# A new table of ranks for the steps of a one-core GLA and RWKV-7 layer

## The chip, the core and the metric

The kernel runs on one core of one Trainium2 chip. The metric is the device time of one execution in microseconds (us); less is better. The engines are PE (matmuls; PEld is its weight load), DVE (vector), ACT (activations), POOL (GpSimd) and SP, whose queue issues the loads and stores. Each engine works through its own queue in order and waits on semaphores for the others.

## The reference, cut to what matters

One decoder layer on 4096 tokens of width 1024: norm, one projection for two groups of heads, a GLA group and an RWKV-7 group, their gated outputs through one output projection, residual and a final norm.

```python
h = _rmsnorm(x, norm_w)
u = (h @ w_in).astype(f32)
gla_u, rwkv_u = u[..., :GLA_IN], u[..., GLA_IN:]
...  # GLA: chunks of 64 tokens, state S_t = diag(a_t) S_{t-1} + k_t^T v_t, o_t = q_t S_t
o = _gla_chunked(q, k, v, log_a.reshape(B, T, GLA_HEADS, GLA_DK))
gla_out = o.reshape(B, T, GLA_VW) * jax.nn.silu(gg)
...  # RWKV-7: token shift, decay w, rate a, normalised key kk, then the delta rule
#   sa = S (-kk);  S = S * w + sa (kk * a) + v k;  y = S r
y = _rwkv7_scan(r_h, decay.reshape(hs), k_h, v_h, kk, a.reshape(hs))
rwkv_out = (y + bonus.reshape(B, T, RWKV_W)) * jax.nn.silu(rg)
merged = jnp.concatenate([gla_out, rwkv_out], axis=-1).astype(x.dtype)
return x + merged @ w_out          # then _rmsnorm(x, final_norm_w)
```

## The kernel before, in words

The tokens are worked through in 8 blocks of 512, the layer's width in tiles of 128. Nine streams of work (generators, one for each kind) describe all of it:

- x loads a block of tokens (`xr<-in_xT_dram`), squares and sums it on PE (`bank<-gtwo,...`), spreads the factors (`bank<-ident,nyg`) and normalises it on DVE;
- w and the output's weights are split into f16 parts: the largest entry is found by transposes (`identb,amW`) and DVE, the matrix is scaled (`wr<-x,scl,wr`) and stored to DRAM (`wdr`), from where it is loaded again later as `wr`, `wg`, `wo`;
- a does the RWKV projections (`bank<-x,wr`) of a unit (a block and one of 4 pairs of heads, so 32 units) and its decays, and makes the inverse of a triangular matrix for every chunk of 64 tokens. For that the matrix goes by the small tiles `Nb`, `nd`, `f`, `Tc`, `td` through DRAM: `nd<-Nb` stores it, `f<-nd` loads it in another layout, POOL builds the inverse row by row with 31 products and 31 sums (`tm<-Tc,f` and `Tc<-Tc,tm`), `td<-Tc` stores that and `Nb<-td` loads it back;
- i multiplies the blocks of the inverse on PE (`Nb,Ta`);
- c is the chain of states, 8 steps of one chunk for a unit, each of them through PE (`ch`), ACT (`us`, `uv`) and DVE (`sv`); e is the same for the last unit;
- d normalises the chain's output and joins the gate (rows by `bcdc` and the like through DRAM);
- g does the GLA part for two pairs of heads in a block, with the row factors `bcdh`, `gbc`, `ki`, and p its projections (`bank<-x,wg` and `bank<-wg,x`);
- o does the output projection and the last norm.

The kernel is built in two passes. `build` runs the streams, and every instruction (a pair of matmuls by `duo` is one) becomes a step with the steps that it depends on (its operands, buffers and PSUM banks); there are 23,692. The steps' numbers and buffers come from the tables `COUNTS` and `STARTS`, the same before and after. Then the steps are issued in the order of a second table, `ORDER`: it is text of packed numbers, and `order()` (line 403) unpacks it to one rank for each step, a permutation. The step of lowest rank whose predecessors are all issued is issued next:

```python
rank = order()
left, can = [len(s.on) for s in steps], [(rank[s.n], s.n) for s in steps if not s.on]
heapq.heapify(can)
while can:
    s = steps[heapq.heappop(can)[1]]
    ...
    s.f()
    for m in s.to:
        left[m.n] -= 1
        if not left[m.n]:
            heapq.heappush(can, (rank[m.n], m.n))
```

So the table alone sets the order of each engine's queue and of SP's. No time is in it: an engine waits for its next step until the semaphores of that step's predecessors have come. Steps on PE have a form (how many of the array's rows and columns a tile takes, and whether it is f32); the costs that the planner has for a change of form, for POOL's sums beside DVE and for a load's landing stand in functions (`forward`, `backward`, `cost`) that rank the steps ahead of time and aren't called when the kernel is built.

Instructions other than the paired matmuls carry the line of the helper `call` (L844), pairs that of `duo` (L905), so views of the profile are read by tiles and not by lines.

Of the kernel before, what the change touches and what calls it, by code (L numbers as in the profile page):

```python
# [2132 lines left out]
```

## Time and profile before

| what | value |
|---|---|
| time, median of 3 runs | 2143.72 us (2143.46 to 2144.85) |
| the profiled execution's own time | 2145.66 us |
| its span | 2143.8 us |
| instructions | 69142 |
| granted PE clock, mean | 0.995 |
| bytes | 322.31 MB by DMA, 150 GB/s |

The span is what the trace covers, the own time is the whole execution's. A row of a timeline has a start, a length, the engine, the line, the operation, the output and its inputs, and in brackets how long the engine stood idle just before and what ended that. A length on PE has a matmul's whole latency in it, so neighbouring rows overlap. Rows of SP's queue give issues; a transfer lands later.

### The profile page before, as it was taken

What the parts mean: (1) busy time and instruction counts of PE and PEld (TensorE: products, weight loads), DVE (VectorE), ACT (ScalarE), POOL (GpSimd) and SP (SyncE); (2) the same over time, 40 slices, a digit from 0 to 9 for tenths busy, and PEclk for the clock granted to TensorE, in tenths of its full rate; (3) what the DMA queues carried; (4) which work ended last, traced back from release to release, by engine and by line L of the source; (5) the groups of instructions that cost most, each with busy time, mean ns of one, the idle gap of its engine ahead of it and who ended that gap; (6) DMA issues with size and microseconds to landing.
All of it is one profiled execution on the core that took longest, in us unless ns stands there. A gap on an engine that the chain in (4) does not pass through costs nothing.

```text
span 2143.8 us, 69142 instructions
## 1 busy us (share of the span) xinstructions
PE 2093.1 (98%) x27880; PEld 1355.5 (63%) x27880; DVE 1615.3 (75%) x3528; ACT 1278.2 (60%) x3356; POOL 880.3 (41%) x2267
## 2 busy tenths in 40 slices
PE   7999999999999999999999999999999999999898
PEld 5656575566756667567676667656676565755565
DVE  8889988668776787678776776757978588776776
ACT  7778786465654656455755457555565565554562
POOL 3663344562253542626433254443334535344500
PEclk9999999999999999999999999999999999999999
DMA  5757756465344653455534654346534465344442
GB/s 172 232 163 249 219 175 179 129 194 171 95 130 132 198 149 109 121 165 173 146 98 126 181 167 129 95 137 187 178 107 112 143 187 165 101 124 133 126 131 85
DMA packets 273701, 322.31 MB, mean 150 GB/s; under 512 B 129844, under 2 KB 135140, under 8 KB 273380
## 3 DMA queue, kind: packets, MB, share of 16 engines
q1 hardware_dynamic: 273380, 317.89, 50.1%
q8 instruction: 218, 3.57, 0.7%
q14 instruction: 103, 0.84, 0.1%
HBM read 272.74 MB, written 45.05 MB: 148 GB/s over the span
## 4 chain that ended last, share of the span: by engine, by line
PE 79%; DVE 12%; POOL 3%; DMA 2%; issue 2%; ACT 2%; SPq 0%; DVEq 0%; ACTq 0%; POOLq 0%
PE bank L905 63%; PE bank L844 9%; PE ch L905 4%; DVE DD L844 2%; POOL tm L844 2%; PE y L844 1%; POOL Tc L844 1%; PE y L905 1%; DVE bk L844 1%; DVE nva L844 1%; DVE x L844 1%; DVE xr L844 1%; DVE Nb L844 1%; DVE mgg L844 1%; DVE nta L844 1%
## 5 line engine op out<-in xcount | busy, mean ns | idle before, releaser
L905 PE MATMUL bank<-x,wr 128*64 128x512 f16 (+1 forms) x6732 | 830.5, 379 | 5.8 <-ACT wr L844 1.9
L844 POOL TENSOR_TENSOR tm<-Tc,f 128x60 f32<-128x60 f32 (+24 forms) x961 | 345.0, 359 | 581.7 <-DMA f<-nd 462.3
L905 PEld LDWEIGHTS <-wr 128*64 128x64 f16 x6732 | 366.8, 111 | 261.6 <-issue 19.9
L905 PE MATMUL bank<-x,wg 128*64 128x512 f16 x3180 | 393.3, 380 | 2.7 <-DVE amW L844 1.3
L844 POOL TENSOR_TENSOR Tc<-Tc,tm 128x60 f32<-128x60 f32 (+24 forms) x961 | 349.9, 364 | 73.6
L905 PE MATMUL bank<-x,wo 128*64 128x512 f16 x2760 | 325.3, 380 | 0.4 <-ACT x L844 0.4
L844 DVE SCALAR_TENSOR_TENSOR sv<-ch,PC,psd 64x64 f32<-64x64 f32 x434 | 122.6, 283 | 205.9 <-PE ch L905 179.2
L844 POOL TENSOR_TENSOR xacc<-xacc,xr 128x512 f32<-128x512 f32 x98 | 134.5, 1372 | 334.0 <-ACT xr L844 188.5
L905 PEld LDWEIGHTS <-wg 128*64 128x64 f16 x3180 | 175.1, 110 | 130.3 <-issue 4.4
L905 PEld LDWEIGHTS <-wo 128*64 128x64 f16 x2760 | 151.0, 110 | 117.6 <-issue 1.4
L905 PE MATMUL bank<-wg,x 128*64 128x256 f16 x3072 | 197.5, 274 | 4.1 <-DMA wg<-wdr 3.9
L905 PEld LDWEIGHTS <-x 128*64 128x64 f16 x3216 | 172.9, 111 | 20.7 <-issue 4.8
L844 ACT COPY us<-ch 64x64 f32<-64x64 f32 x496 | 101.9, 205 | 134.4 <-PE ch L905 117.4
L844 ACT COPY uv<-ch 64x64 f32<-64x64 f32 x496 | 102.0, 206 | 88.0 <-PE ch L905 80.5
L844 ACT ACTIVATE psd<-sv,PC 128x128 f32<-128x128 f32 x248 | 98.8, 398 | 84.7 <-DVE sv L844 61.5
L844 ACT ACTIVATE sa<-bank,mu_s 128x512 f32<-128x512 f32 x104 | 71.3, 685 | 53.2 <-PE bank L905 47.4
L844 DVE COPY_PREDICATED Nb<-mc,bank 64x512 f32<-64x512 uint8 x128 | 93.0, 729 | 5.8 <-PE bank L844 3.5
L844 DVE COPY_PREDICATED DD<-mc,bank 64x512 f32<-64x512 uint8 x128 | 93.2, 729 | 2.5
L905 PEld LDWEIGHTS ch<-uv,bk 128*64 128x64 f32 x992 | 67.4, 137 | 39.6 <-ACT uv L844 6.6
L905 PEld LDWEIGHTS ch<-sv,DD 128*64 128x64 f32 x992 | 65.6, 136 | 39.3 <-DVE sv L844 13.8
L905 PEld LDWEIGHTS ch<-us,Nb 128*64 128x64 f32 x992 | 66.7, 137 | 37.2 <-ACT us L844 6.5
L905 PE MATMUL ch<-uv,bk 128*64 128x64 f32 x992 | 71.5, 223 | 3.5 <-ACT uv L844 3.2
(359 smaller groups left out, 3538.4 us busy)
## 6 DMA issues: line engine op xcount, KB each, us to landing
wr<-wdr SPq DMA_DIRECT2D x254, 256.0 KB
wg<-wdr SPq DMA_DIRECT2D x182, 256.0 KB
xr<-in_xT_dram SPq DMA_DIRECT2D x176, 256.0 KB
wo<-wdr SPq DMA_DIRECT2D x116, 256.0 KB
f<-nd SPq DMA_DIRECT2D x128, 128.0 KB
x<-in_wt_dram SPq DMA_DIRECT2D x29, 512.0 KB
wdr<-wo SPq DMA_DIRECT2D x17, 512.0 KB
rn<-bcda SPq DMA_DIRECT2D x64, 128.0 KB
```

Source lines behind the costliest of these rows:

```text
L844: put(t0, self.name, d, lag, cols, tiles, tab, outs, ins, lambda: f(*a, **kw))
L905: nc.tensor.matmul(x, lhsT=l, rhs=y, start=start, stop=stop)
```

## The change

The text of `ORDER` is replaced. `COUNTS`, `STARTS`, all steps, their costs, buffers and code are the same. Unpacked and compared for each queue, with the share of steps whose place in the queue is another:

| queue | steps | moved | mean shift, places | largest shift, places |
|---|---|---|---|---|
| PE | 12,968 | 4198 | 1.27 | 108 ahead, 49 back |
| DVE | 3528 | 1561 | 0.87 | 71 ahead, 12 back |
| ACT | 3206 | 1165 | | |
| POOL | 2261 | 252 | | |
| SP (loads and stores) | 1729 | 890 | 1.05 | 12 either way |

On PE the number of neighbours of different form goes from 590 to 589. Places that the text below speaks of, by their times in the profile before:

- 12.08: the first spread of the norm on PE, 5 places later, behind four pairs of statistics.
- 39.5: the DVE step that makes `glr`, 5 places later.
- 1799 to 1805: on SP's queue the four loads `f<-nd` go ahead of `bcdh<-nyg` (1801.18), `gbc<-bcdh` (1802.85), a `wr` load (1803.28) and `ki<-bcdh` (1803.71); the last `nd<-Nb` one place ahead.
- 1978.64: a chain step on PE, ahead by several matmuls.
- 2007.11 and 2010.99: two `wg` loads, each one place back, behind `td<-Tc` (2022.62), which goes two places ahead.
- 2022 to 2023.7: a few matmuls of `wr` from later on are put ahead of those that use the two `wg` loads.

```diff
@@ -55,168 +55,166 @@
 PUT_OFF = 1.0
 FILL = ()
 ORDER = (
-    "c-qZf2b^40)qiE`_L9x+rWevkAPFgu5FnxVCZIF{L7IRcibxYt1mu(AhYA)zQBV+3L{Moef`Sw&A`qmv0D(X
...
+    "c-qx{2bf(|)%Gd3PA{1xGwD5{q(BOU0HKB^y+{>7K;%OO1w=X`A0P+<f&w<Ah@yxnpdbR$1XOyJ4k5HaN
...
```

More of the change, by code (lines that the diff above doesn't have):

```diff
@@ L217 @@
[L217 to L219 removed]
+    "c-qx{2bf(|)%Gd3PA{1xGwD5{q(BOU0HKB^y+{>7K;%OO1w=X`A0P+<f&w<Ah@yxnpdbR$1XOyJ4k5HaNYBjN`OnIE*K^<5*{9sOGxGg;o|Aj$-gD2{XYaLFeb-u(9LMp3qbK<HLU6dj`)ZH6;AjqxRl)T(30^b7"
@@ new lines @@
+    "F*G=C!1ar`XD&E8gU>d_?@Gb@$Ae>0aC8KJcLlG@f@7=TeHLT<cX0SPUw)gzd%0H;?^g%!3n|9wSw4Fr`0e_^Ypvznd~nFU+k@jj!FitL96A0Fe3!vzbMV<D<D7GY<HF#)(ZTB>xbCIF-;?kxw_>hj94)~yFF5YS"
+    "Gs<VL1@GH}SDCxpg7-4t4Z-no@V+K^-6%M8uCkaDc|R4;DDP(k$653oLn7v=2j}?4cQy1`H$AhgTh@5q;q>0eZ}s~zpovkz@jRYU=;aN(ACCDhVvKKMedQdXmmzrnHlAJ1e<gU|7`zS+j`K0LiNW!5@P0Ure?oAK"
+    "1daN5t;d|ne7+T&zd`W2G3M=sfJo)}zJ)Qj(R0c14P56Utl#H@<DTGsC(-R{nopVAeQDq2g8weF?86-PRHb{dsY3eaBLmutJ7-KV);BP|iCBk><vz98H=c0}6M7HkRQCQ+#&|tkOI~*kjwzV46M~a33tsQT+U0Og"
@@ new lines @@
+    "6TX+f8}VMozf*92TX4Zsf_oet{Qbk=b^qXXT5t%Tc`5jQcQ?G}WUT4Q#u{Y$F!#BL&y@~#1&u8PA8V!kQ49Ji;u(+ZC*B;j{x$SIKLFPko<0Vj%?*x!7`%LAJge-jq1b<$;k!@p>_Q{I!CYmr#wthF!#!Mlw;o={"
+    "2S0k%4bNK<9Cw$(b8<NHSld=w=Mng>#_~+cJ7j&n1A3{$eOW&Iz(PMd)~rF_V~H2c1WjH-veND6eXq2f#l7UdcVON<l3B6`rr_LR_?@ibwZXAR@LfxaakNx8?hk3+WDM5_$BDsbEMJ!4oJk3ER|7hD6*|Q4jBA^}"
+    "Q<{4}I8Wr{N5QMei^-t9`6LVF{8_=E^7!3y$eTyK{@tVIF(u}i|0gA1w;kW=hp}w~edM8FE@VFb7R=8h!K>_(D}vV_2d~ctuO~sKvdop=?=3t%_)hlEeC)MfK}Qmu=+DNUlDS_K!52+krGfUl2VKL1uG#^a{9}Cf"
@@ new lines @@
+    "<>37`c#dm&LV2$|O7#wx<k#=}i8t31pWx?^>mMWZ2KqcP;(qh+Te;5dIA=)2y`uQayTR{fLr-!cBlii8n}WaZ$J#{wK128006gfLgt?JDx@~a$nRIzRHUn>N#q~vxx+*xf1pnuAZ;`PY_uB?K-gvCJ=#KI_$TF_>"
+    "3glWg;haY3Ybwu$f4quk?7;7L#@OWip}~KLKsIfU-yIkn7bMJIK4y&T6D>Up+d^f~EzoD>{a}3eQt<jkoG<cc1m3sNb!OnaF?c>7YcdGDQGT}r?K78T+eM(KkHF78>?wKwd@0>NPP2zx3vDDFOCkSU@bb8Gb?w)y"
+    "LLagn*9G@I9P2OhbzE?4271xo502Qgao61p{OvZJ_dWbZ?4@C_n;z%`56d|NE9-2upwCc4pJj;m$>+1N*B>{Y>Ac|Y(;y2<uu%um{`AR5;X*I7J+GI7F86}Iu{&his)YI77IxxR7)u@bMD7fZGw58|FQ3EpbSzs0"
@@ new lines @@
+    "$C-VYQ<=L3{j@&Q>HQ`N>)0Rnn+9E7d8QA3D*S0_cklVGOQ|QXwCEUa3SC<F_MNaTAH;P|gKV2kw*K}ho-J$eGdV<Wx)6Gi_;>!+6Y8IO{zTA56ZEiuVhqRQ-omGw;gfSMwx35jkw?Ct#SyZZb&Cy2R_JH9CeVBa"
+    "^LrH5(X;42a{oUV*BOt!dARZUQu;d&yV(UVu<1!2=1HDU^oy-hu1(xAs2}Kh23`*?mF;60>oL$b7eK!o<(B6t51p(Be60cR#diKnaNLgh6us#%vZYifR=Y-hHDY7clf986KDj&I-vfV}OTJFq9#`3t18-KnKMxw#"
+    "^X6OjoQHGTFvf+@FVqGXT0N!|(x=**hY;^P5V{KQ(FVMVA7XR(>YAZ%HDM2luJ$I4t;Hh8ry8I6DP(@04$)O_!|#Od?h-zabvQDD_v`{1d$A|{Hy(2;Ja4?kzC8l-<Qp=~HdeXjEaUreG;W#e>w|N4gx^Db&ZD89"
@@ new lines @@
+    "|1dc5)9%m?&cat9zr8Yn57>P56Y0K<*z<pf54f3RY!7spS%?`-120ng-xmDxM$r6x(6oH_3$am+Ig{sF82s@y(H9IEVvbYvCZV;hgCCyW9qq623^|j<-q{6ns`gKobUitqhHq43AL|>otn!Hi$!;v-`9^_9=8Um7"
+    ";n-UIqVl^^S%&x+PY?8!8sfoOiopzpUG*~PMLv57e)v|RJsHFKVhcikh&-yLIT&Zm(Q~vGQxbUOv)Cs*FPj?YTt#}6JjWL;-z!g(Ik_D3w7o&E<{qAqQm?Oxu><ZS`&wTAD*On1T=(Ak7I}Fh=1yZM%Cm>k{f@zB"
+    "e=Wtw!F=$CYhZU=g)#XN=gM4P4SsnX_*D<tjC&D%irm?{)H^05V|v`J+(z203R${KKiVH#S;m*f*Y*K)<4rI(FN1Gi(v>bw8F$Ej-@*9ou`2yhYGaCx(G{%WTsPb!r$Qesf)-a3y)<LZeT&{&7onroMa-YZaD=wT"
@@ new lines @@
+    "LbkDAWxB+ONr!kD@j#E{R1fxk3*=)C&$UGS#=&>vXxzhb{(K|e*+RO}P~z<wiVv4a2lBAKd3@eV&t3x`rur=R4Nlk#=ZvH=?-?9>V~^|J9s=HVE#~17(z$12td}E>UaZ1aA57zwYyOMYS7SHR5PO#KormW<m2A<E"
+    "p*MEovqq9V9`Sx1=b`xgFZiAM=uZ$|I_B0Rdpye5q35(3u@;T{z5+ck1E15S&<8y7=SE#~Yv|qb{@9*)ouC$<t+vRJ4D?OKEy!oz1?|qnT-6)DnS*)IvCbmju6daLsGZ;g*)Mqgb@2KX@e!ot4a&=#i4J8R9)ZlC"
+    "f^`&H*u}W!uVDkLPhaHvD@048>+TU8`v%81Wj_R8{H81Xz8!I$pNk$(zl-xhWg~3oiS+(q_<e_9pPdidmAQW?c(Xa_+g^gtVu-QNMiNidx%vWh&RNhGRtgUQw&nYHrY4KMGo7A6Fb}Gyi48v`f%fBk35^N97!Pv9"
@@ new lines @@
+    "jIj(h?z5eR#|XyZ7U+M9e~|d+_hQzL=d;yVH`CTXlH#ik7X9ip@{>=Gz#}y!%-JXlkCb`81GeEe@R`K1u3OpD^9XDX;a`7|*mFQbE5V~=&&>dzS%i6Mf}C0p?_WcVQTF>g!TY&*wkxvsd1@iMneBA(W&AB*HaF%%"
+    "{Y1V$Ao%<GTsW_C%}s*8PtS$>p&8d%pROZz?mpzpx)SlZG4SW8zNz~98pNqHINmL#*Egc{r-HGzrp;W${nyHDgRVq(-Jk4}29o2ogtzG-Kde6MrO;~z<NGG^eXNavL&nC%U0N}(i=lI{{p6Bg%%@{m!aNl~-|CON"
+    "1J_eO-Yyv519-L^WJ6R;{ZgDi#Tb`9OOE7MwR-Z$@G(xrb>~2rkbi3+%l>H0=}?l{;|+|^7<@0!@f&<L7IwetfLZ7cwHA47`f5ztyElbzJ_jB=j(%5<>+0MMCOxQV_=o2N|2;<gM4m_dXg|htYzRKHUmtwrm0&FV"
@@ new lines @@
+    "l=gKk;rP~o=FD@NjX3KZ@L}PN!uy2|z6{wj3w&5&Ya(}Zqz{zvej9h-Vn-teFfR4Y3eV^DItlv0H!%-tdz{x9zTeOd{cCRk2a%)s^85KYUWHxc!Uysn$f_lX0aSDC2FRHXL(YreV|UR0zO-LX4?f!q_aBbuzKHN$"
+    "eHlX*e04;3PmkycFN5ALfKN38{<=TWrQkoW4o=#tE7YTpb^8|c9iP%Cp>dE)jQP%C9yZ1p<@K@z{c1GDI`gz=8z^RA`|T{~FnO{mHUeJxQ1}-%0mkD31J^3{;myGxo0Q7<um-ZD8)3tVZuLm;<!_<)-#WmtW5x3o"
+    "D!_8;`9AG~8J2x##uv;u)_PcTS&yZqvW(cA&KnegA<_8sBKW>N3-8Whj+cRVd<oB(1(xZs;Pn~U62gOjL4MDIg>GhGZB=i{AQmNSc#cI!$n`;Hc@}-!gAelCaz7lK1oUyeA3mGLG2Sq+_Zh5H4|EIm>3W8rMq^~^"
@@ new lines @@
+    "(;jE6+j@jko*4Y->#$X;#a&J?`~_Ls>tc5uKz=2emv3Wl?~n85;`0%>Rs-$3RoGV?lPwbFe?H<0_28iyngfy1$0PPL8T9rG;wuwre)7a48xbeVgB}a;4P8a!Y9Ku*8!=A>L;tJC`i%vxjt1{}x;v!*m4-Yo#`w2t"
+    "Equ5x2K&k55FdrC{dRa(jWaw5Ix5h7kB5J0FfbTXq2Iq9(9cQ0JI%uU{hH>sjqLJkLDPpv(9gUo`Jb%Y_Q80LD24ZVz>W7G)WpnD95%wEbrBjq0W#vUK49n@V`33a6<(``Z07>#Y~P4yXfW=TF=*{v*m<61u57-j"
+    "Vih><IE)*Q)r<H(ZVg`o%}uwg;Y#q&w}ByO55CwBwzcXGzcciY?*xCJN&Ghl9x)sC-v+?Pcri3ug6+K${5h>XIubmg9k@yleB&kf*motq@oa>@Vx$p&ttB5=mT>WE!;ipR=$?He;<`I0j6F{}y=VB2ZS*-6@_Z(~"
@@ new lines @@
+    "?}BghE&Og1jH@2sZBIP88|OF!U~7%<r|TTrhu_RjdEUYBNqd+Jp~-J_hWOX-x*`4i1hVmJ*yxH=mHluk=2CEoN>g{Iw2k8Qqm3>4V-ED2sbVhmnu7VM4~`?;Q2%}%d2l{t(yt62GCZX(+{}%62RS1@$2@tYLz}<-"
+    "6nsSWwpP+ha)!-d8%r1A(v;r_kGdCnjQAQ}qu9x6@a-&kO<jUa%A~O8GVsmiNv~19@m}!xNO}&R{E|ho8(i4Ng5mraIFi%c-uaTAWlTfqUOOAS;uE^xbA-Q|N&I<B$fa!{N7m+DkPofh;*-ok*Xc0UDnpoB7doxb"
+    "!AGUu{?;RnYfi?!eS<b?@cGeXx5|D!trW_W83sMtu!C`H8-?NU2%oVP*7FGby&AOC0=r=Y(Cl#7w3k2!9D}(YhFoB;0{p&btgqrK@5dU>g-qTT`u5uKLdLEpK0nQv%a<U#UHGZjGv-R|p!<p6%r$I^+vxf`S@?ua"
@@ new lines @@
+    "2bWmaHz>#EEYObXv=3r_@`xb`?L8$i7R>J#h__~qeW1Cz--wytMX-N!z}NT||7DK&RJEA)op7y}kv}os4P!$kvbk@kTmw@l^T@VQACB^j$@u(NF>$~RQs_*BVUx7r)lcAkvtSoX?xpx?&VUbh3h}Zv*!#kh&m>)@"
+    "2YhC`|8lMX`xnj6*017v2UK{z?47Id{$=<%YlBG=-Sjof`J?(F*VZ-aBMd{1@rIzOZwBvW@9k*G<toO+lRpFwHx5%$v|#OPA!F`EEc9K_{|e||&thy3Vq7JICZB-cZ8z|Tt!a#!>pc{5nD1+1Fq**&rxI^dfBeTJ"
+    "FXxa?E*mkws-N7{54nFkM120|K;Z4|g}TN)!F$Q?obIm6H@pgSKHFmAI5z~7f0!G}y)OVa(I3yLwDPA?7;DxV4O<Y7QDoFc#_!I9U6zGEMsNl4dO0xP`&58$N)tCY&-h#Pq5BBG!}k6d@>9$sjO3+|X<5QCzZns;"
@@ new lines @@
+    "@htu+*U<Yq$kx0IcKJ+Pe;2YHFM_UhHTkC$JNYztf!gkjb1RZxZxG#k4Zg1<zk)tvH*$Pk<R0-eJw-mV*@jGcm~{S`5o_=d(p9u}3d^GxDEEAD#QuDbV*aYXEDQ!c-Ye6K;%W9upc&hm6^wJd7#S+qw%x$nr;!bQ"
+    "FXa`xkj2cCmcc)->y$D0m<xMrIIW9bV<=%L-=^yhHuhvI{Z4HZ!Cn2;@bzk*p^m53;wy83YpJ7oxB0`~GW3HHMsDMaw04uCbYrOvM0Hx011Fy(pEH*A%#t4793xNjz&!5*9=bE+s?wy+_Ztbka!8eWW)8elWvj^f"
+    "D<$qjpY@QQZOdQe99gZ+GoO4Z!rQh;c#e7_ANoT>SGV~MCSVN)ffv*hHlrQqbb%IUTl`jU4v?OB&;VR>hUK$8VQY;hdYnX9Ni(Ks;+zyCAiB~~!NN;C?rt|3V^s}SU~+J;m$2TlKZao~P95MpVewH-fDOJ0_^4^a"
@@ new lines @@
+    "|A+F{qHsQLjK9h^a-5zCCU{Rb{7m@Nea1brDfILsFjp$`8<a-@!=X5fM#{CT1vXxI=h4Bs{xK8kJL|0upYNmKZ}Hu=0J|zVldV1B`hOpLZ#`V^733GF-tl>S{wC$hECFwo^=vJb@$-#@(VuR}*9~Lr4xi>^By5ao"
+    "_KvK@|6*<D0i(fwsILcaUhE3(hgIaaFHqiRl8w}E_|(}JYM~k!QNEhn`XSF^ZT?y*#Lyq_mg^6w>=hdKU3-3nNAX`Xo}VWkJ=@5IFJf=$-yMekCW}4yj^Vr77QbzW{wd@CAUH>K`fZSh#(9}C{tu~Uh<T`eR!8{)"
+    "{EVt=tTghEbEG@uQux)b0S>JhdXbM@v@F$oDB`&fMIPC<c#gGtcd2(ghIO*6Q?6r}CtW#5`kJiIEx^vmeSQF*vo*~x>uVznnjK`pNvd9^dY|ms-=(Ov66e>@YdwtXoT&PY<ew;RHkb>+LmW$b@CdS9IInmnY+IeL"
@@ new lines @@
+    "BT;fv{0v`%oYGtm{{Bh$l-BloiQrk>BeAhc8PpWxS2VHfHHh2vkj<xg;rC)s%^_ZJKWc|9>4R-7I_SsU;W|hk=Hmxg77tJG6DltGGRnz1JK?$ZfX<}$!z$4ECYHGt`7|GU|7^jlYkgHGT|LN#3UoYMeqFWoed;UB"
+    "87eyQb)0>~rb@upujQv*p?n+(AIR{8d%Ox?can}`i=FHTTQCcGt@&MCm$loFOBwP*$?L?GA)fi?h4^)lo;+vKHKsz|n)TbF;(Cpg6T$xbMG0}iMKS*Vit_FQAtVnjeu)vlSD#uaV~{?gaiqb^=={!ilIu+W!T4V3"
+    "XM5wk)e*IHpN+vvR%$zGzQTI}!K|Mx_wc$HI&Xs^BZ`EtQ@cm}6#If#e7nNE9EC@`p%m5v8|sEwkp+-@J*Xk}c1nA#L_Uv3+GAQ{PQQE3$a_=%q;&Qn>7pwQT%$SmVgz17k9~qKZq1hQ4`%>dHphwXO~Ey?RrmZ5"
@@ L220 @@
+    "249~afuFdG)*>oDLvm=(Mt!Rtft6URtGm5x3^maDE~Q>(W^Pv2f?+aiYU_MmjreJ2DU|W^VQ1{+rt8^NpWt5>J?EQF*zac}JjZ^)@e!`^r&4eGKWkt)`U6+k5u>wv2G)Re@okK}#Mg~{jQ++w=A6pv*JV=V;Cha|"
+    "53uTcKILu<r8#)Zk{|9y@KQ5Zo@>FGF+c7V%k%dt@$`(5S5TzSHvx_zL(imsz(x36|E`5DmL-`~guYlq*RF-m;(_+Gmdqm3D+l8_7#lap(7$rf4T?^=KU^lk#`KN)FkT9~rq;0KGSJN*!L!c5INR_HgCM&HLtbjl"
+    "nKnA_8l0znChJk#qs1xrL&_rlGLrU84e~S!bY2^HH`~mUoZdb2wC4J&M$OvM7W`q0B_GaB$h9_K^A*}^%@~J=`>!M{Q;}+5X^o6!geR1F`hUnTCt?"
 )
```

276 lines of the change are left out of this document (114 added, 162 removed).

## The prediction

> **What bounds the kernel now.** I read the page's first parts, then a table of stretches, then the waits of the matmul engine, then the timeline at the places where the table of ranks moves something.
>
> ```profile
> span 2143.8 us, 69142 instructions
> PE 2093.1 (98%) x27880; PEld 1355.5 (63%) x27880; DVE 1615.3 (75%) x3528; ACT 1278.2 (60%) x3356; POOL 880.3 (41%) x2267
> PE 79%; DVE 12%; POOL 3%; DMA 2%; issue 2%; ACT 2%; SPq 0%; DVEq 0%; ACTq 0%; POOLq 0%
> 0.00:214.00 214.00, 188.93 (x2366) 124.72 (x2368) 183.89 (x473) 163.17 (x349) 100.89 (x252) 0.98 0.66 204
> 214.00:428.00 214.00, 209.28 (x2804) 134.55 (x2800) 176.54 (x398) 141.08 (x376) 95.17 (x251) 1.00 0.59 176
> 428.00:1929.00 1501.00, 1497.28 (x20008) 967.85 (x20006) 1101.92 (x2273) 871.47 (x2332) 630.45 (x1643) 1.00 0.49 144
> 1929.00:2036.00 107.00, 101.05 (x1298) 63.46 (x1294) 75.06 (x161) 49.97 (x144) 50.99 (x119) 0.98 0.45 131
> 2036.00:2090.00 54.00, 53.44 (x810) 36.13 (x808) 41.13 (x126) 36.45 (x112) 0.00 (x0) 1.00 0.48 130
> 2090.00:2143.80 53.80, 43.15 (x614) 28.82 (x610) 36.81 (x102) 16.07 (x46) 2.82 (x4) 0.93 0.26 85
> ```
>
> The first three lines are the span, the busy times and the chain that ended last; the others are stretches with their length, then busy time and instructions of PE, PE's loads, DVE, ACT and POOL, PE's granted clock, the DMA share and GB/s. PE is the bound: idle 2143.8 − 2093.1 = 50.7 us. The stretches say where: 25.1 before 214, 4.7 up to 428, 3.7 in the 1501 us after that, 6.0 up to 2036, 0.6, and 10.7 in the tail. The same instructions run in the new order, so only these 50.7 us and PE's price of changing form are to be had, while a worse order can add idle time anywhere.
>
> ```profile
> PE bank L905 <- DMA wg<-wdr: 4.1, 2, 3.9
> PE ch L905 <- ACT uv L844: 3.2, 4, 1.0
> 187.58 1.09 PE L844 MATMUL bank<-ident,bk 128*128 128x128 f32 x8
> 188.61 0.62 PE L905 MATMUL bank<-x,wr 128*64 128x512 f16 x4
> ```
>
> Two of the waits (total us, times, longest): most are of this kind, a few times under 1 us, spread over producers. The two timeline rows (start, length) show a change of form: from the first of eight transposes to the f16 matmul behind them go 188.61 − 187.58 = 1.03 us, the visit and its two changes together, so one change costs a part of half that; 0.1 us is my estimate.
>
> **The change, part by part.** It replaces one table, the rank of each of the 23,692 steps. Decoded, 4198 of PE's 12,968 steps change place, mean 1.3 places; 1561 of 3528 on DVE, 1165 of 3206 on ACT, 252 of 2261 on POOL and 890 of 1729 loads and stores on SP's queue. Nothing is added or removed. Changes of form on PE go from 590 to 589: **−0.1 us**.
>
> *Start.* The first spread of the norm (from 12.08 below) moves five PE places back, behind four pairs of statistics; by the first row eight such matmuls take 0.60 us. DVE's normalisation waits for it, and behind that lies the weight split that PE waits for at 20.68:
>
> ```profile
> 8.92 0.60 PE L905 MATMUL bank<-gtwo,uv 128*64 128x1 f32 x8 [0.70 <-ACT uv L844]
> 12.08 1.10 PE L905 MATMUL bank<-ident,nyg 128*64 128x128 f32 x8
> 18.92 1.70 DVE L844 SCALAR_TENSOR_TENSOR wr<-x,scl,wr 128x1024 f16<-128x1024 f32 x1
> 20.68 0.64 PE L905 MATMUL bank<-x,wr 128*64 128x256 f16 x4 [1.79 <-DVE wr L844]
> 13.30:20.60 7.30, 5.18 (x70) 4.07 (x70) 7.30 (x21) 5.49 (x14) 2.59 (x4) 1.00 0.94 309
> ```
>
> The split keeps its place on DVE, so the 1.79 us wait grows by 0 to 0.6. I take **+0.5**, near the upper bound, since DVE was busy for all of the 7.30 us before (last row: length, then PE, PE's loads and DVE) and has no gap that swallows it.
>
> *Waits that go.* For each wait of PE I took how far its producer moves ahead (places times the lengths of the steps passed), less PE's own shift, capped by the wait. 22 places give something, 7.5 us in all: 1.3 before 30 us, 1.1 in the chain steps at 136 to 163, 1.6 at 175 to 226, 0.4 at 312, 0.9 between 1307 and 1799, 1.5 at 2010 to 2015, the rest after 2070. One of each of two groups and the largest:
>
> ```profile
> 162.50 0.34 PE L905 MATMUL ch<-uv,bk 128*64 128x64 f32 x4 [0.71 <-ACT uv L844]
> 2010.41 0.34 PE L905 MATMUL ch<-uv,bk 128*64 128x64 f32 x4 [0.65 <-ACT uv L844]
> 2013.77 0.49 PE L844 MATMUL bank<-DD,bk 64*128 64x128 f32 x2 [1.15 <-DVE bk L844]
> ```
>
> The steps around the large waits at 42, 57.6, 153, 158 and in the tail stand as before. A relieved chain step is followed by the next one of the same chain, whose producer is then late instead; so I count two thirds: **−5.0**, bounds 0 and −7.5.
>
> *Waits that come.* The same reckoning the other way finds 20 places (45 links) where a producer falls behind its use on PE, first at 3.7 us, last at 2013.8, 12.8 us in all. The largest two:
>
> ```profile
> 1978.64 0.28 PE L905 MATMUL ch<-us,Nb 128*64 128x64 f32 x4
> 1977.14 0.73 ACT L844 COPY Nb<-bank 32x256 f32<-32x256 f32 x2
> 39.52 0.62 PE L905 MATMUL bank<-glr,guw 128*64 128x512 f16 x4 [0.73 <-DVE pw L844]
> ```
>
> The chain step at 1978.64 moves 1.9 us ahead on PE while the copies that it reads end at 1977.87: about 1.3 us of new wait. At 39.52 the producer on DVE moves five places back: 1.1. I count these whole (2.4). The other 10.4 assume that a producer starts late by all that was put ahead of it; but in the long middle DVE is idle 1 − 1101.92/1501.00 = 27% of the time and ACT 42%, which takes up most shifts of one place. I count a fifth, 2.1. **+4.5**, bounds +1 and +12.8.
>
> *SP's queue at 1800.* SP issues in order, and an entry that isn't ready holds all behind it:
>
> ```profile
> 1799.42 0.43 SPq L844 DMA_DIRECT2D nd<-Nb  x1
> 1801.18 0.57 SPq L844 DMA_DIRECT2D bcdh<-nyg  x1
> 1802.85 0.34 SPq L844 DMA_DIRECT2D gbc<-bcdh  x1
> 1804.23 0.38 SPq L844 DMA_DIRECT2D f<-nd  x1
> 1805.13 3.33 SPq L844 DMA_DIRECT2D f<-nd  x3
> 1807.85 0.75 DVE L844 SCALAR_TENSOR_TENSOR go<-go,gnh,gbc 128x512 f32<-128x512 f32 x1
> 1811.16 0.75 DVE L844 SCALAR_TENSOR_TENSOR gbc<-gbc,gus,gep 128x512 f32<-128x512 f32 x1 [1.11 <-ACT gep L844]
> ```
>
> The four loads of f are moved ahead of bcdh and gbc. The first f issued 4.8 us after the last nd; the last nd goes out at about 1797.9 now, so the f's run from 1802.7 and gbc follows 3 to 5 us later than before. DVE's use at 1807.85 stood 5.0 us after its load; it slips by up to 3.6, of which the idle 1.11 at 1811.16 takes a part: 0 to 2.5 us for the chain step behind it on DVE, of which PE has other matmuls to fill most: **+0.5**.
>
> *SP's queue at 2007.* Here the largest single wait of the late stretch changes hands:
>
> ```profile
> 2007.11 4.20 SPq L844 DMA_DIRECT2D wg<-wdr  x2
> 2022.62 0.37 SPq L844 DMA_DIRECT2D td<-Tc  x1
> 2025.43 0.89 SPq L844 DMA_DIRECT2D wg<-wdr  x2
> 2023.35 3.99 PE L905 MATMUL bank<-wg,x 128*64 128x256 f16 x70
> 2025.92 5.28 DMA wg<-wdr
> 2031.25 2.96 PE L905 MATMUL bank<-wg,x 128*64 128x256 f16 x26 [3.92 <-DMA wg<-wdr]
> 2027.00:2031.00 4.00, 0.33 (x8) 0.06 (x2) 0.26 (x1) 0.00 (x0) 0.00 (x0) 0.96 0.79 241
> 2031.00:2036.00 5.00, 4.75 (x62) 4.28 (x64) 2.83 (x15) 0.22 (x1) 0.00 (x0) 0.69 0.07 14
> ```
>
> The store td of POOL's last sum, ready only at 2022.6, moves ahead of the first two wg loads (2007.11 and 2010.99). They can then go out at 2023.0 and 2023.4, though PE wants them from 2023.4 on, after the few matmuls put ahead. The second two loads still follow at about 2025.6. Two loads issued together took 5.28 us after the second issue, with nd and f beside them; so the first pair lands between 2026 and 2028.7 and PE waits 2.6 to 5.3 us there, then works some 3.7 to 4 us on it (the row at 2023.35) and finds the second pair landed. The old 3.92 us wait goes. The half clock moves with the wait: 0.69 of full speed over 5.00 us is 1.55 us lost once, before and after. Resumed work on the second pair starts between 2029.7 and 2034, against 2031.25: −1.5 to +2.8, and +5 if PE is slowed on both stretches. I take **+0.3**.
>
> *POOL.* Its sums stay whole, with the same steps. By its row (busy us and mean ns; then the idle time before and what ended it) the engine stood idle 462.3 us for loads of f, so a shift there lies beside PE's work except at the store just told:
>
> ```profile
> L844 POOL TENSOR_TENSOR tm<-Tc,f 128x60 f32<-128x60 f32 (+24 forms) x961 | 345.0, 359 | 581.7 <-DMA f<-nd 462.3
> ```
>
> **Sum:** −0.1 + 0.5 − 5.0 + 4.5 + 0.5 + 0.3 = +0.7 on the profiled execution's own 2145.66 us (span 2143.8 and 1.86 around it): 2146.4. That execution is 1.94 us above the median of the runs, so 2146.4 − 1.94 = 2144.4.
>
> **Rivals.** A bound for all: a change within 0.2%, 4.3 us, cannot be told from none here.
>
> *Relief without new waits.* If all 7.5 us come and of the new waits only 1.3 at 1978.6, with 1.0 of the start and SP kept: −0.1 − 7.5 + 1.3 + 1.0 = −5.3, **2138.4**. For it: at 22 places the producers do come ahead, and DVE and ACT have idle time; against it: the largest early waits aren't touched.
>
> *Slower by SP's queue alone.* The pair of wg loads held behind td until 2022.6 is the one mechanism; it decides if the pair lands after 2028 and PE has nothing else ready. At its upper bound of +5.0 with the other terms as summed (+0.4): **2149.1**. For it: 5.28 us of landing and idle POOL and ACT in that stretch; against it: the old wait in the same place, which it replaces.
>
> *The half clock after new waits.* Rows above show 0.69 in the 5 us behind a wait of 3.92, and 1.00 wherever the waits are under 1 us. If three of the new waits join to some 4 us (1978.6, the pair at 2023, the start), each costs 1.55 us besides: 0.7 + 3 × 1.55 = +5.4, **2149.1**. Against it: the new waits are 1.3 us and less but for one. [...]
>
> *The change does nothing.* The shifts average one place, and the middle has 3.7 us idle in 1501: between 2143 and 2145.5.
>
> **Chances.** Forecast with its close kin (no measurable change) 0.50; relief 0.28; SP's queue 0.12; half clock and the new waits in full (0.7 + 8.3 = +9.0, 2152.7, the upper end) 0.10. Faster than 2139.4: 0.28. Slower than 2148.0: 0.22. The low end takes half of the faster cases off below 2137 (relief in full with no new wait: −7.1); the high end, 2150, leaves out the new waits in full. The likeliest case alone spans 2140.5 to 2147.5.
>
> **What would show it.** In the profile after: PE idle before 214 us still about 25; no wait of 3.9 us on wg at 2031 but one of 2.6 to 5.3 at about 2023, with td<-Tc ahead of wg in SP's rows and the half clock behind it; gbc's load 3 to 5 us later than f's begin; a chain wait of about 1.3 near 1977; the waits at 162.5, 220.9, 2010.4 and 2013.8 gone. I am wrong if idle time in the middle changes by over 3 us, or if DVE's or POOL's busy time does: then steps met each other otherwise than the shifts of places tell.

## The result, and the profile after

The changed kernel takes 2164.7 us (median of 6 runs, 2156.9 to 2166.1) against 2144.3 for the kernel before; by the means of the runs (2163.4 and 2145.6) the ratio is 1.0083, 95% interval 1.0064 to 1.0102. It is slower by 0.8%, clear of the noise; the forecast was no measurable change, 2144.4 with a range from 2137 to 2150. The profiled execution took 2164.26 us with a span of 2162.4, so 18.6 us more span than before. Single executions of one order differ by some us (2143.5 to 2150.7 in six of the kernel before, 2156.9 to 2166.1 in six of the changed one), so below a ratio is from the timed runs, and a span or a wait from the one profiled execution.

The page after, its first parts, and the stretches, with the columns as before:

```profile
span 2162.4 us, 69086 instructions
PE 2099.6 (97%) x27880; PEld 1358.3 (63%) x27880; DVE 1608.2 (74%) x3528; ACT 1274.7 (59%) x3356; POOL 893.6 (41%) x2267
PE 75%; DVE 10%; POOL 6%; DMA 4%; issue 2%; ACT 1%; SPq 1%; DVEq 0%; ACTq 0%; POOLq 0%
0.00:214.00 214.00, 188.15 (x2324) 122.75 (x2326) 179.14 (x471) 160.15 (x343) 97.13 (x244) 0.97 0.66 203
214.00:428.00 214.00, 205.28 (x2748) 132.24 (x2744) 170.83 (x385) 140.09 (x376) 98.60 (x257) 0.98 0.58 174
428.00:1929.00 1501.00, 1490.68 (x19881) 963.34 (x19878) 1093.98 (x2264) 864.23 (x2315) 637.05 (x1622) 1.00 0.49 142
```

In the chain that ended last POOL went from 3% to 6% and DMA from 2% to 4%. PE's idle time went from 50.7 to 62.8 us (2162.4 − 2099.6), and its busy time grew by 6.5 us with the same instructions, which fits more of them running at half clock (mean granted clock 0.991 against 0.995). Laid side by side by place in PE's queue (the start of the n-th step after, less that of the n-th step before), the delay grows like this:

| stretch, time before | delay gained, us |
|---|---|
| 0 to 229 | +1.3 |
| 229 to 257 | +8.1 |
| 257 to 1320 | +2.3 |
| 1320 to 1343 | +2.7 |
| 1343 to 1764 | −0.8 |
| 1764 to 1834 | +3.6 |
| 1834 to 1993 | −0.2 |
| 1993 to 2060 | +1.0 |
| 2060 to the end | +0.5 |

Small entries say little: k1, k2, k4 and e8 (below), which have the old order there, gain 2.0 to 2.9 us between 300 and 500 alone. So it is a few places, and the largest was in no part of the prediction. Read it backwards, from PE's wait to its cause. The timelines of PE, DVE, ACT, SP and POOL of the changed kernel:

```profile
248.36 0.32 PE L903 MATMUL bank<-identb,om 128*64 128x128 bf16 x2 [4.82 <-DVE om L842]
247.54 0.69 DVE L842 SCALAR_TENSOR_TENSOR gg<-gg,bank 128x512 f32<-128x512 f32 x1 [4.53 <-ACT gg L842]
246.21 0.63 ACT L842 ACTIVATE wo<-xr 128x512 f32<-128x512 f32 x1 [8.24 <-DMA xr<-in_wo_dram]
242.42 0.91 SPq L842 DMA_DIRECT2D xr<-in_wo_dram  x2
241.38 0.37 SPq L842 DMA_DIRECT2D td<-Tc  x1
240.69 0.66 POOL L842 TENSOR_TENSOR Tc<-Tc,tm 128x8 f32<-128x8 f32 x1
202.84 0.24 POOL L842 TENSOR_TENSOR tm<-Tc,f 128x31 f32<-128x31 f32 x1 [18.50 <-DMA f<-nd]
197.05 0.50 SPq L842 DMA_DIRECT2D f<-nd  x1
192.45 1.30 SPq L842 DMA_DIRECT2D f<-nd  x3
```

PE waits for the largest entry `om` of the output weights; DVE's step before it in the queue waits for ACT, ACT for the load `xr<-in_wo`, and that load stood in SP's queue behind the store td of POOL's last sum until 241.38. POOL's last sum ended at 241.35. It had begun at 202.84, after the fourth load of f, which had been put behind two stores of split weights, and it took longer than before. The same places before:

```profile
192.07 1.75 SPq L844 DMA_DIRECT2D f<-nd  x4
198.60 0.24 POOL L844 TENSOR_TENSOR tm<-Tc,f 128x31 f32<-128x31 f32 x1 [15.77 <-DMA f<-nd]
232.06 0.22 POOL L844 TENSOR_TENSOR Tc<-Tc,tm 128x8 f32<-128x8 f32 x1
234.48 0.33 SPq L844 DMA_DIRECT2D xr<-in_wo_dram  x1
234.91 0.48 SPq L844 DMA_DIRECT2D td<-Tc  x1
```

So POOL began 4.2 us later and took 4.8 us longer (38.5 against 33.7). Before, td was not held up by POOL: the last sum ended at 232.3, and td went out at 234.91, behind the load of 234.48.

The wait also cost clock. By stretches of the changed kernel:

```profile
243.00:248.40 5.40, 0.58 (x8) 0.10 (x4) 0.88 (x4) 1.91 (x5) 0.73 (x5) 0.92 0.97 287
248.40:253.40 5.00, 5.00 (x40) 4.14 (x42) 4.67 (x12) 2.67 (x5) 0.00 (x0) 0.50 0.57 173
253.40:260.00 6.60, 6.60 (x58) 3.31 (x56) 5.41 (x11) 1.30 (x4) 0.00 (x0) 0.93 0.46 142
```

The clock was 0.50 for 5.00 us and 0.93 for 6.60: 2.50 + 0.46 = 3.0 us lost, which with the wait of 4.82 makes 7.8 of the 8.1.

The other three places have the same form, a store or small transfer that SP waits for, and a load behind it. Near 1336 (SP, then PE), from 1805 on (DVE, SP, PE), and near 2040 (SP, PE, and PE's clock in a stretch):

```profile
1335.82 0.37 SPq L842 DMA_DIRECT2D td<-Tc  x1
1336.28 1.74 SPq L842 DMA_DIRECT2D wg<-wdr  x2
1340.89 1.28 PE L903 MATMUL bank<-wg,x 128*64 128x256 f16 x20 [2.60 <-DMA wg<-wdr]
1811.22 0.75 DVE L842 SCALAR_TENSOR_TENSOR xr<-xr,nwx,xacc 128x512 f32<-128x512 f32 x1 [3.27 <-DMA xr<-in_xT_dram]
1816.24 1.71 SPq L842 DMA_DIRECT2D f<-nd  x4
1823.32 0.32 SPq L842 DMA_DIRECT2D gbc<-bcdh  x1
1827.25 0.89 DVE L842 SCALAR_TENSOR_TENSOR go<-go,gnh,gbc 128x512 f32<-128x512 f32 x1 [4.08 <-DMA gbc<-bcdh]
1832.38 0.34 PE L903 MATMUL ch<-sv,DD 128*64 128x64 f32 x4 [1.39 <-DVE sv L842]
2039.87 0.37 SPq L842 DMA_DIRECT2D td<-Tc  x1
2040.34 1.00 SPq L842 DMA_DIRECT2D wg<-wdr  x2
2044.05 6.99 PE L903 MATMUL bank<-wg,x 128*64 128x256 f16 x74 [3.67 <-DMA wg<-wdr]
2044.00:2049.00 5.00, 4.96 (x48) 4.27 (x50) 0.00 (x0) 0.00 (x0) 0.00 (x0) 0.50 0.76 217
```

The last three SP and PE rows are the exchange that the prediction described: td first, then the two wg loads, PE's wait of 3.67 us ahead of the first pair, and none ahead of the second.

### The profile page after: what moved, and what is told of

Its sections match the earlier page's. It is cut to its first block, busy times and chain, and to the rows that moved or that the text cites. A ratio compares the mean times of both kernels' runs of the same rounds, so it can differ in the third digit from the quotient of the medians.

```text
span 2162.4 us, 69086 instructions
## 1 busy us (share of the span) xinstructions
PE 2099.6 (97%) x27880; PEld 1358.3 (63%) x27880; DVE 1608.2 (74%) x3528; ACT 1274.7 (59%) x3356; POOL 893.6 (41%) x2267
## 4 chain that ended last, share of the span: by engine, by line
PE 75%; DVE 10%; POOL 6%; DMA 4%; issue 2%; ACT 1%; SPq 1%; DVEq 0%; ACTq 0%; POOLq 0%
PE bank L903 60%; PE bank L842 9%; PE ch L903 4%; POOL tm L842 3%; POOL Tc L842 3%; DVE DD L842 1%; PE y L842 1%; PE y L903 1%; SPq L842 1%; DVE bk L842 1%; DMA f<-nd 1%; DVE nva L842 1%; DVE mgg L842 1%; DVE x L842 1%; DVE nta L842 1%
## 5 line engine op out<-in xcount | busy, mean ns | idle before, releaser
L842 POOL TENSOR_TENSOR Tc<-Tc,tm 128x60 f32<-128x60 f32 (+24 forms) x961 | 362.6, 377 | 74.2
L903 PE MATMUL ch<-sv,DD 128*64 128x64 f32 x992 | 71.6, 224 | 3.4 <-DVE sv L842 3.2
```

Source lines behind the costliest of these rows:

```text
L842: put(t0, self.name, d, lag, cols, tiles, tab, outs, ins, lambda: f(*a, **kw))
L903: nc.tensor.matmul(x, lhsT=l, rhs=y, start=start, stop=stop)
```

## The experiments

All runs use the same steps and differ in the order alone. Theory A was that the loss is made in SP's in-order queue, theory B that it is made by the order on the compute engines. Ratios are to the kernel before, timed beside each run.

| run | order | span, us | ratio, 95% interval |
|---|---|---|---|
| (changed kernel) | new everywhere | 2162.4 | 1.0083, 1.0064 to 1.0102 |
| e1_sp_before | new, SP old | 2151.0 | 1.0031, 1.0017 to 1.0045 |
| e2_sp_after | old, SP new | 2155.5 | 1.0070, 1.0046 to 1.0095 |
| e3_td_back | new, 3 td back | 2153.5 | 1.0051, 1.0031 to 1.0072 |
| e4_f_back | new, 1 f back | 2155.8 | 1.0037, 1.0024 to 1.0050 |
| e5_five_windows | new, 40 steps of SP old | 2148.3 | 1.0029, 1.0017 to 1.0041 |
| e6_pe_only | old, PE new | 2159.8 | 1.0071, 1.0056 to 1.0086 |
| e7_dve_act_only | old, DVE and ACT new | 2161.8 | 1.0070, 1.0049 to 1.0090 |
| e8_last_td | old, last td ahead | 2148.8 | 1.0010, 1.0000 to 1.0020 |
| s1 | new before 180 us | 2146.8 | 1.0018, 1.0003 to 1.0032 |
| s2 | new 180 to 262 us | 2151.5 | 1.0053, 1.0036 to 1.0069 |
| s3 | new 262 to 1780 us | 2147.0 | 1.0015, 1.0000 to 1.0030 |
| s4 | new from 1780 us | 2144.5 | 1.0031, 1.0019 to 1.0044 |
| k1_f_only | old, f group near 192 new | 2149.9 | 1.0011, 1.0000 to 1.0022 |
| k2_td_only | old, td near 235 ahead | 2146.0 | 1.0002, 0.9991 to 1.0013 |
| k3_f_restored | new, f group near 192 old | 2158.2 | 1.0046, 1.0030 to 1.0062 |
| k4_wg_first | old, wg ahead of td near 2022 | 2143.7 | 0.9992, 0.9983 to 1.0001 |

**Which queue.**

```diff
-queues of PE, DVE, ACT, POOL, SP: new
+e1: PE, DVE, ACT, POOL new; SP old      e2: PE, DVE, ACT, POOL old; SP new
```

> The new order on PE, DVE, ACT and POOL; SP's queue of loads and stores alone in the old order. Theory A (the loss is made in SP's in-order queue: stores td that wait for POOL's last sum, and loads of f and gbc, are put ahead of loads that PE needs): the jumps of the new order at 244 (8.1 us), 1328 (2.8), 1800 to 1832 (3.9) and 2022 (about 1 net) go, and of 2164.7 about 15.8 us: 2149, between 2145 and 2154. Theory B (the loss is made by the order on PE, DVE, ACT and POOL: producers late, POOL's sums meeting other DVE steps): SP's queue matters little, 2160 or more, and the wait of 4.8 us at 248 stays.

> The old order on PE, DVE, ACT and POOL; SP's queue alone in the new order. Theory A: slower than 2144 by 8 to 13 us (2152 to 2157), with an idle time of PE of some 3 us and half clock behind it near 243, since the fourth load of f still goes out late and td still holds the load of the output weights. Theory B: no more than 3 us slower than before, up to 2147.

With SP's queue old, the ratio falls from 1.0083 to 1.0031, about 11 us, and the wait at 248 is 0.07 us. With SP's queue alone new, the old kernel loses 0.70%, 15 us by the ratio, some more than theory A gave and far from the 3 us of theory B. At 244 PE waited 1.37 us there, less than the 3 that theory A gave. The largest wait is the exchange near 2024 again, without the cover that the new order of PE put ahead of it:

```profile
2035.56 0.42 PE L901 MATMUL bank<-wg,x 128*64 128x256 f16 x2 [6.11 <-DMA wg<-wdr]
```

**Single moves in the changed kernel.**

```diff
 # e3, SP's queue at three places
-td, xr(x), xr(wo), xr(wo)   td, wg, wg   td, wg, wg, nd x4
+xr(wo), td, xr(x), xr(wo)   wg, td, wg   wg, wg, td, nd x4
 # e4, SP's queue near 192
-f, f, f, wr, wdr, wdr, f
+f, f, f, f, wr, wdr, wdr
```

> The new order, with three stores td put back on SP's queue behind the loads that they overtook: one near 241 behind the first load of output weights, one near 1336 behind one wg load, one near 2040 behind two wg loads. Theory A: the 4.8 us wait at 248 and the half clock behind it go (8.1 us); at 1340 less than 1 us comes back, since one wg load still follows td; the 3.7 us wait at 2044 goes, and a wait at the second pair of wg comes back (net 1 us): 2155, between 2152 and 2158. Theory B: 2162 or more.

> The new order, with one load on SP's queue put back: the fourth load of f (issued at 197.05, behind two stores of weights) goes ahead of the other three, as in the old order. Theory A: POOL's sums of that unit start 3 us earlier than 202.84, td at some 238 instead of 241.4, and the wait at 248 falls from 4.8 to about 1 us without half clock behind it: 2158, between 2156 and 2161. Theory B: POOL's lateness comes from its sums running longer beside DVE, so td moves by less than 1 us: 2163 or more.

Both gained about what they should in time (ratios 1.0051 and 1.0037), but not in the way that was expected. In e3 the first load of output weights went out at 234.75, the second, which stood behind td in the old order too, at 243.76: a wait of 3.84 us stayed, and most of what e3 gained it gained near 2040, where its delay by the place in PE's queue falls by 4.4 us. In e4 the wait at 248 went, but the load wr stood behind four loads of f instead of three, and a new wait came:

```profile
248.80 0.25 PE L899 MATMUL bank<-identb,om 128*64 128x128 bf16 x2 [3.84 <-DVE om L838]
201.52 1.92 PE L899 MATMUL bank<-x,wr 128*64 128x512 f16 x8 [2.62 <-DMA wr<-wdr]
```

The first row is e3, the second e4. So a place on this queue is worth what stands around it, and groups have to be put back as a whole.

**Five groups.** e5 puts the five groups of neighbours back (7, 3, 2, 25 and 3 steps); DVE/ACT and PE alone are e6 and e7, and e8 is the last td in the old kernel.

```diff
 # e5, SP's queue of the changed kernel, near 192, 235, 1317, 2007
-f,f,f,wr,wdr,wdr,f   td,xr(x),xr(wo)   td,wg   td,wg,wg
+wr,f,f,f,f,wdr,wdr   xr(wo),td,xr(x)   wg,td   wg,wg,td
 # and 25 steps from 1791 to 1807 (nd, Nb, xr, bcdh, gbc, ki, f) in the old order
 # e8, the old kernel: wg, wg, td becomes td, wg, wg near 2007
```

> The new order everywhere, with five groups of neighbours on SP's queue (40 of its 1729 steps) put back to their old order: the loads of f near 192, td and the output weights near 241, td and wg near 1336, nd, f and gbc near 1800 to 1820, td and two wg near 2040. Theory A (these groups carry SP's whole part): as the run with all of SP's queue in the old order, a span of 2150 to 2153, ratio to before 1.003 to 1.004; no wait of 4.8 us at 248, of 2.6 at 1341 and of 1.4 at 1832; the 3.9 us wait of the old order on the second pair of wg is back. Theory C (the loss on SP's queue is spread over its 231 changed groups): a span of 2156 or more.

> The old order on DVE, ACT, POOL and SP; PE's queue alone in the new order. What the run with SP in the old order left over is 7.2 us of span. Theory P (it comes from PE's steps put ahead of their producers, the new waits of the prediction): 3 to 6 us above the old kernel, a span of 2147 to 2150. Theory V (it comes from the order of DVE and ACT): within 1.5 us of 2143.8.

> The old order on PE, POOL and SP; DVE's and ACT's queues in the new order. Theory V: 3 to 6 us above the old kernel, a span of 2147 to 2150, most of it at the start (0 to 130 us) and near 1289, where DVE ended a wait of 2.8 us. Theory P: within 1.5 us of 2143.8.

> The old kernel with one move: the store td near 2022 goes ahead of the two wg loads at 2007 and 2011. Theory A: a wait of 5 to 6 us near 2024 in the place of the 3.9 us at 2031, with half clock behind it: 1 to 4 us slower, a span of 2145 to 2148. The rival, that the two waits are the same and only change places: within 0.5 us of 2143.8.

e5 gives 1.0029, the same as all of SP's queue put back: the order of 40 of SP's 1729 steps carries 1.0083 − 1.0029 = 0.54%, some 11.6 us, two thirds of the loss. At 243 PE no longer waits, and at 2034 the old wait is back (from its list of waits: 3.7 us on wg):

```profile
235.76 7.29 PE L899 MATMUL bank<-x,wg 128*64 128x512 f16 x66
242.89 0.22 PE L899 MATMUL bank<-identb,om 128*64 128x128 bf16 x2
PE bank L899 <- DMA wg<-wdr: 3.7, 1, 3.7
```

e6 and e7 refuted both theories on the rest. PE's new order alone loses 0.71%, DVE's and ACT's alone 0.70%, while all of them and POOL's together lose 0.31% (e1). So neither is the culprit by itself. That each without the other meets producers or consumers that were moved fits waits like these two, e6 and then e7, which stand in no other run; it isn't shown further:

```profile
1188.32 0.43 PE L839 MATMUL bank<-crs,bones 128*32 128x128 f32 x8 [2.25 <-ACT crs L839]
166.03 0.25 PE L901 MATMUL bank<-identb,amW 128*64 128x128 bf16 x2 [2.47 <-ACT wo L840]
```

e8, three steps, made a wait of 4.70 us near 2031 (5 to 6 were expected) in the place of the old 3.92; the ratio, 1.0010 (1.0000 to 1.0020), is 0 to 4 us and agrees with theory A without deciding it.

**Stages.**

```diff
-new order on all queues, 0 us to the end
+s1: new where the old profile stands before 180 us   s2: 180 to 262   s3: 262 to 1780   s4: from 1780
```

> The new order on all five queues where the old profile stands before 180 us, the old order after it (785 steps move). Theory A (the loss is made at a few places, each by itself, and adds up): the jumps of the changed kernel before 180 us make +0.5 to +2.5 us: a span of 2144 to 2147. Theory I (the loss is one of interplay: the new order of one stretch suffers from what another hands on): no more than noise here, and the four stages together fall well short of 18.

> The new order on all queues from 180 to 262 us, the old order elsewhere (476 steps). Theory A: the fourth load of f is late, POOL's sums end late, td holds the load of the output weights and PE waits 4 to 5 us near 247 with half clock behind it: +7 to +9 us, a span of 2151 to 2153. Theory I: less than half of it, up to 2147.

> The new order on all queues from 262 to 1780 us, the old order elsewhere (5696 steps, the largest share of the change). Theory A: the wait on wg near 1328 (2.8 us), 0.9 near 1140 and small ones: +3 to +5 us, a span of 2147 to 2149. Theory I: within 1.5 us of the old kernel.

> The new order on all queues from 1780 us on, the old order before (1458 steps). Theory A: gbc late behind f's loads (1 to 4 us near 1800 to 1820), td ahead of two wg loads (+1 us near 2022), +0.4 in the tail: +3 to +5 us, a span of 2147 to 2149. Theory I: within 1.5 us of the old kernel.

The four losses, 0.18, 0.53, 0.15 and 0.31%, add up to 1.17%, with an interval of about ±0.3, against 0.83 ± 0.19 for the whole: within that the places add, and no stage is seen to need another. s2, 476 steps, has the wait of 5.22 us at 249 to itself; s4 has 1.24 us at the chain step (sv) and 3.79 at wg; s3 has 2.09 at wg near 1332. s1 has one that the prediction had no place for, an ACT step `vt` two places later:

```profile
105.50 0.94 PE L839 MATMUL bank<-qi,ki 64*128 64x128 f32 x12 [1.70 <-ACT vt L839]
```

**Which move makes the wait at 248.**

```diff
 # k1 (old kernel) and, reversed, k3 (changed kernel): SP's queue near 192
-wr, f, f, f, f, wdr, wdr
+f, f, f, wr, wdr, wdr, f
 # k2 (old kernel): SP's queue near 235
-xr(wo), td, xr(x)
+td, xr(x), xr(wo)
 # k4 (old kernel): SP's queue near 2007 to 2026
-wg, wg, td, nd, nd, nd, nd, wg, wg
+wg, wg, wg, wg, td, nd, nd, nd, nd
```

> The old kernel with one group of 7 neighbours on SP's queue in the new order: three loads of f ahead of a wr load near 192, the fourth behind two stores of split weights. Theory F (the late fourth load of f, through POOL's sums, is what makes the loss near 244; td's new place only decides which half of the output weights is held): POOL starts that unit's sums 3 to 4 us later, td goes out near 239, PE waits 1 to 2 us for wr near 198 and 2 to 4 us near 243: a span of 2148 to 2152. Theory D (td's place ahead of the load is what makes it): within 2 us of 2143.8.

> The old kernel with one group of 3 neighbours on SP's queue in the new order: td near 235 ahead of the first load of output weights. Theory F: POOL is in time, the load goes out 1 to 1.5 us later, PE waits less than 1 us near 243: a span of 2143.5 to 2145.5. Theory D: a wait of 3 us or more near 243, a span of 2148 or more.

> The changed kernel with that group of 7 put back to the old order. Theory F: the waits at 200 (0.4) and at 248 (4.8, with half clock behind it) go: 8 us off the span of 2162.4, 2153 to 2156, td still ahead of the load. Theory D: the wait at 248 stays above 3 us, a span of 2160 or more.

> The old kernel with one move on SP's queue in the other direction: the second pair of wg loads (issued at 2025.4 and 2025.9, ready by 2021.9) goes ahead of td (2022.6) and of the four stores nd behind it. Theory A (what waits in SP's queue holds the loads behind it, and PE pays): they go out near 2020.2 and 2021.9, land before 2027.1, the wait of 3.9 us at 2031 and the half clock behind it (1.55 us) go: a span of 2138 to 2140, ratio 0.997 to 0.998, faster than both kernels. The rival (the landing is bound by the traffic of nd and f): the wait only falls to 2 or 3 us, a span of 2142 to 2143.

Neither move does it alone: in k1 and k2 PE doesn't wait at 243 at all. Theory F fell in k1; k3 lies between the two, where the wait went from 4.82 to 2.69 with td still ahead. The traces of ten runs in one table show why (start of POOL's sums of that unit, time to the end of the last one, issue of td, PE's wait for `om`):

| run | POOL starts | POOL takes | td | second xr(wo) | PE waits |
|---|---|---|---|---|---|
| before | 198.6 | 33.7 | 234.9 | 237.1 | 0 |
| k1 | 200.3 | 34.3 | 234.6 | 236.6 | 0 |
| k2 | 198.1 | 34.3 | 232.4 | 236.5 | 0 |
| e1 | 199.3 | 36.1 | 235.5 | 237.5 | 0.07 |
| e5 | 199.6 | 36.9 | 236.4 | 237.6 | 0 |
| e2 | 202.3 | 35.0 | 237.3 | 238.9 | 1.37 |
| k3 | 201.6 | 38.1 | 239.8 | 241.3 | 2.69 |
| changed | 202.8 | 38.5 | 241.4 | 243.0 | 4.82 |
| s2 | 203.0 | 38.9 | 241.9 | 243.5 | 5.22 |
| e3 | 203.9 | 38.8 | 242.7 | 243.8 | 3.84 |

There is a slack. POOL was done at 232.3 in the kernel before; up to a td at 236.4, 4 us later, PE waits 0.07 us at most, beyond it a us of td costs nearly a us of PE, and with the longer waits the clock besides (0.68 over the 5 us behind 2.69 in k3, 0.50 behind 4.82 in the changed kernel). (e3 waits less than its td tells: only the second load stands behind td, which makes it 6.1 us instead of 7.0 from td to PE's step, and PE itself came 1.4 us later. e4 is left out, since PE came late there.)

Three things use the slack up: the late fourth f, POOL's own part, and td ahead of the loads. Each without the other two is hidden: k1 has the first, e1 and e5 the second (with the new order of PE, DVE and ACT), k2 the third. Two of them show, f and td with all of SP's new order in e2 (1.37 us), POOL and td in k3 (2.69), and all three make 4.82. Their sizes are less sure. The group of f moves POOL's start by 1.7 us from before to k1 and by 1.2 us from k3 to the changed kernel, and the rest of the 4.2 isn't told apart. POOL's own part is 2 to 5 us: 72 instead of 67 steps, five small ones moved in, and products and sums of 499 ns on average in the changed kernel instead of 451 in the one before. No run moved POOL's queue alone.

k4 shows the mechanism in the other direction. Freed from behind td, the four wg loads were out before it and PE ran through:

```profile
2009.71 15.07 SPq L840 DMA_DIRECT2D wg<-wdr  x4
2025.23 0.37 SPq L840 DMA_DIRECT2D td<-Tc  x1
2025.93 10.43 PE L901 MATMUL bank<-wg,x 128*64 128x256 f16 x188
2024.00:2031.00 7.00, 7.00 (x122) 6.04 (x120) 5.65 (x15) 0.10 (x1) 1.63 (x10) 1.00 0.56 130
2031.00:2037.00 6.00, 6.00 (x106) 5.63 (x102) 2.25 (x12) 2.48 (x7) 0.00 (x0) 1.00 0.49 142
```

The old wait of 3.92 us and the 0.69 clock behind it are gone: 5.5 us there by the place in PE's queue, of which 1.6 were given back by 2055. The ratio of 0.9992 (0.9983 to 1.0001) is 0 to 3.6 us faster, less than the 4 to 6 that were expected; it is the best order that ran, though not clear of no change.

## Why the prediction was wrong, point by point

**The step that failed** is the part on POOL: "a shift there lies beside PE's work except at the store just told". SP's queue was costed at two places, 1800 and 2007, while td goes ahead of a load at 235 and 1319 as well, and the sum nowhere asked how late POOL itself would be. The reason given, 462.3 us of idle time for loads of f, is a total over the span; in this one unit POOL had 4 us to spare. By the old trace td's new place at 235 looks free, since POOL was done at 232.3; k2 shows that it is, in the old kernel. But the same table also makes POOL start later and take longer, 9.1 us at its last sum, and then every load behind td inherits POOL's delay, the second load of output weights, which stood behind td before too, among them. A place on the queue has to be priced with the producer's new time. Measured: 8.1 us at 248, 2.7 near 1340, neither in the sum, which had +0.8 for all of SP's queue where e5 shows some 11.6.

**SP's queue at 1800** was the right mechanism, mis-sized: +0.5 with bounds 0 and 2.5, against 3.6 on the trace. gbc's load went out 7.1 us after the first f (1816.24 to 1823.32), not 3 to 5, DVE stood 4.08 us for it and PE 1.39. Missed was a load a little ahead of it, `Nb<-td`, moved 12 places up, behind which a load `xr` held DVE for 3.27 us; PE's next wait for DVE, at 1813.5, was 1.46 us where it had been 0.57.

**SP's queue at 2007** came as described, a wait of 3.67 us within the 2.6 to 5.3 given and none on the second pair; +1.0 on the trace against the +0.3 taken. The half clock was priced at 1.55 us; it was 0.50 for 5 us this time, 2.5 us.

**Waits that go** gave 2.5 us, not 5.0: the waits at the places counted fell from 9.4 to 7.0 us. Those in the chain at 136 to 163 went, but 220.9 (1.04 to 0.96), 2010.4 (0.65 to 0.72) and 312 stayed, and 2013.8 grew from 1.15 to 1.63. **Waits that come** gave about 2.6 us, not 4.5: of the 20 places only five show more wait than before (16.7, 27.2, 107.3, 765 and 2013.8), and the largest that was counted whole, 1978.6 (1.1 us by its own rows, not 1.3), none at all; the first, at 3.7, began 2.0 us later and had made it good by 50 us. Both terms were too large and the difference, +0.1 instead of −0.5, was right by cancelling. **Start**: +0.5 forecast, +1.3 by 229 us, but not by the wait that was costed: that at 20.68 fell from 1.79 to 1.59, while the one at 57.6, held to stand as before, grew from 1.35 to 2.41. By 158 us the delay was +0.5, and the rest came with a clock of 0.66 from 158 to 163, where the kernel before had 1.00. s3, with the old order in this stretch, has the same +1.3, so that the term can't be told from none. **Form changes** can't be seen at 0.1 us.

**The signs of being wrong** that the prediction named came: idle time of PE from 428 to 1929 went from 3.7 to 10.3 us, POOL's busy time from 880.3 to 893.6 and DVE's from 1615.3 to 1608.2.

**The rivals.** "Slower by SP's queue alone" named the right queue and the right mechanism at the wrong place and price (+5.0). "The half clock after new waits" did come, 3.0 us behind the one at 248. That waits under 1 us leave the clock at 1.00 didn't hold even before: it was 0.50 from 64.6 to 68.0, behind waits of 0.78 and 0.23 us. Nor does it take 4 us: behind waits of 2.62 us (e4, at 201.5) and 2.69 us (k3, at 246.7) the clock was 0.66 and 0.68 over the next 5 us, 1.6 to 1.7 us lost, and behind 2.60 us (changed kernel, at 1340.9) it was 1.00. What makes the difference isn't shown; the last section has the numbers.

**What stays open.** With the five groups put back 0.29% are left (0.17 to 0.41), some 6 us; s1 holds perhaps half of it. Part of it is seen (`vt` 1.3 us in e1 and e5, 2013.8 about 0.5), the rest is spread over small waits that differ from one execution to the next (2.0 to 2.9 us between 300 and 500 where the order is the old one, k1, k2, k4 and e8), and no run tells them apart.

## What to carry to other kernels

On a queue that issues in order, price a store not by when its data was ready in the old trace but by when it can be ready in the new order, and list every load behind each such store: there lies the risk of a reordering, more than in the shifts of single steps on a busy engine. Look for the slack: here 4 us of it hid each of three changes, and two or three together went through it. Parts of an order that were chosen together can't be judged apart: PE's order alone and DVE's and ACT's alone each lost 0.7%, together with POOL's 0.3%.
